# Two diffusion-transformer layers on one core: 16-bit sums of squares, the first FFN scales in one go, and three other paces

## The chip, the cores and the metric

One core of one Trainium2 chip. The metric is device time in microseconds (us) of the whole program, one launch. Engines are named as in the profile: PE (TensorE matmuls), PEld (its weight loads), DVE (VectorE), ACT (ScalarE), POOL (GpSimd), SP (SyncE, which issues most DMAs).

## The reference

Two layers over 1024 latent and 256 context tokens, width 1024, all in float32; in layer 0 the context tokens go through the same steps. Each layer normalizes and modulates, projects, runs windowed attention and a 2-D Fourier mixing side by side, projects out, and ends in a SwiGLU FFN of hidden width 2816.

```python
def fourier_mix(u, w_four):
    ...
    mixed = jnp.fft.fft2(ug, axes=(1, 3), norm='ortho').real.astype(u.dtype)
    return jnp.einsum('bngc,gcd->bngd', mixed, w_four).reshape(B, N, FOURIER_WIDTH)

def swiglu(h, w_gate, w_up, w_down):
    return (jax.nn.silu(h @ w_gate) * (h @ w_up)) @ w_down

def reference(...):
    for i in range(DEPTH):
        ...
        h = modulate(rmsnorm(x, norm_pre_mix[i]), sh1, sc1)
        p = h @ w_in[i]
        ...
        attn = windowed_gqa_with_context(q, k, v, kc, vc, sink[i])
        four = fourier_mix(u, w_fourier[i])
        mix = jnp.concatenate([attn, four], axis=-1) @ w_out[i]
        x_mid = x + g1 * rmsnorm(mix, norm_post_mix[i])
        hf = modulate(rmsnorm(x_mid, norm_pre_ffn[i]), sh2, sc2)
        x = x_mid + g2 * rmsnorm(swiglu(hf, w_gate[i], w_up[i], w_down[i]), norm_post_ffn[i])
        ...
```

## The kernel before

**Tiling.** Activations lie transposed, channels on the 128 partitions, tokens along the row, in two blocks: A and B of 640 tokens in layer 0, two of 512 in layer 1 (latent tokens alone). Float32 accuracy comes from splitting each operand into a high and a low part: three 16-bit matmuls (hi·hi, lo·hi, hi·lo) stand for each product of the FFN. The up product also uses a seven-product scheme on 2×2 halves, so each FFN weight pair needs four sums of its quarters, scaled by a power of two and split.

**FFN weights.** `load` reads the two 512 KB halves of one gate or up weight into the pool `raw` (four buffers). `start` adds, on ACT, the squares of each half (`junk`, L441; the sums land in `ss`). `factor` sums `ss` over the partitions with two float32 matmuls against ones (`wsum`, L420) and turns the result into the scale `sp` with three small DVE instructions (`power`, L410 to L412). `sums` then makes the four operands: ACT the high part (`wa` or `ww`, L457), DVE the low part (L458), with four additions of quarters between the second and the third (L469 to L472). The first four pairs, eight weights, are made ahead by `ahead`: for layer 0 beside its attention, for layer 1 beside the down product of layer 0. They are written to DRAM (`wc`) and read twice by `ffn_up`. The other weights, from pair 4 on, are made inside `ffn_up`, where `ready` calls `factor` and `wino`.

**What sets the order.** The program is written as generators. `mix` takes from several of them in turn: each has a total, and the next step comes from the one whose done share of its total is smallest. A larger total makes a generator run earlier. A scheduler then orders each engine's instructions, with program order as priority; engines work their rows in the resulting order, and PE, DVE, ACT, POOL and SP wait for each other at semaphores.

**Places that matter here.** In the attention of each layer three or four generators run together: `fill` (the rest of the projection, the Fourier mixing, the first half of the output projection; total FILL), `attn` (total ATT), in layer 0 `work` (the modulation matmuls, reading `wada`) and `early` (`ahead` of layer 0). In `fourier` each pass of first products (`v`, L955, and `vc`, L1003) is split by ACT and DVE (L909, L910) before the second products (`pq`, `fc`). At the start of `ffn_up`, block 0's products of the first four pairs run while `side` makes block 1's operands: `postnorm` of block 1, its statistics (`ssq`, then the matmul `nps`, L665), the spread of the scale over partitions (`rps`, L687), and `prenorm` (`hn`, then `ffn`, L743 and L744). Later in layer 0's `ffn_up`, `mod(0, 1)` makes layer 1's modulation on DVE (`wm`, L643). The down product (`acc<-…,wd`, L1215) converts its weights on the way: `wd` by ACT (L1207) and DVE (L1208), from the same four `raw` buffers.

## Time and profile before

| | us |
|---|---|
| median of 3 runs | 2600.11 (2595.58 to 2609.46) |
| the profiled execution | 2605.76, its span 2604.0 |
| PE busy | 2412.8 (93% of the span) |
| DVE busy | 1790.5 (69%) |
| ACT busy | 1347.3 (52%) |
| POOL busy | 196.9 (8%) |
| DMA | 390.06 MB, mean 150 GB/s |

The stages of the span, from the first and last matmuls of each line: up to 185 us the modulation and the first projections of layer 0; to 545 its attention, with Fourier's first products from 333 on; to 603 the second output projection; to 1158 the FFN up product; to 1505 the down product; then layer 1: projections to 1572, attention to 1863, output projection to 1915, up product to 2345, down product and the tail to 2604. Busy times of different engines overlap. A row of waits names the engine that waited and what released it. The granted clock is a share of full speed.

### The profile page before, as it was taken

To read this page: it belongs to the slowest core of one execution; us is meant where nothing else is said; L and a number is where in the kernel's file an instruction comes from. 1 tells how busy PE (TensorE), PEld (TensorE's weight loads), DVE (VectorE), ACT (ScalarE), POOL (GpSimd) and SP (SyncE) were. 2 spreads that over 40 slices of the span, in tenths; PEclk is the share of its full clock that TensorE was granted. 3 is DMA by queue.
4 is the path that set the end of the run, shared out by engine and by line. 5 is a ranking of instruction groups with operands and counts; after the bars stand their busy time and mean duration, and the time that the engine had idled before them with its cause. 6 is when DMAs were issued, how large, how long until landed. Compare 5 with 4: busy or idle time off the path is not lost.

```text
span 2604.0 us, 44237 instructions
## 1 busy us (share of the span) xinstructions
PE 2412.8 (93%) x17370; PEld 1935.6 (74%) x17370; DVE 1790.5 (69%) x3474; ACT 1347.3 (52%) x2587; POOL 196.9 (8%) x204
## 2 busy tenths in 40 slices
PE   7989988998989999988998989999999999999997
PEld 5878777896667677655665779988777888884486
DVE  5687686777556887765568478787767477765485
ACT  4565556567334445434456336566574355545473
POOL 0212110010000000000000024310000000000000
PEclk9989989999989999998999989999999999999998
DMA  8433323477634333357557141101396521236374
GB/s 299 152 109 103 106 74 108 162 239 278 209 131 146 106 108 122 122 195 269 198 192 273 64 141 61 45 25 33 109 333 237 180 82 66 81 103 232 117 256 128
DMA packets 152769, 390.06 MB, mean 150 GB/s; under 512 B 16976, under 2 KB 33776, under 8 KB 152560
## 3 DMA queue, kind: packets, MB, share of 16 engines
q1 hardware_dynamic: 143344, 372.55, 42.2%
q10 hardware_dynamic: 9216, 14.68, 1.6%
q8 instruction: 136, 2.23, 0.3%
q14 instruction: 73, 0.60, 0.1%
HBM read 322.41 MB, written 64.76 MB: 149 GB/s over the span
## 4 chain that ended last, share of the span: by engine, by line
PE 48%; DVE 10%; issue 4%; DMA 4%; ACT 3%; SPq 0%; POOL 0%; POOLq 0%; ACTq 0%; DVEq 0%
PE p L1084 21%; PE acc L1215 17%; PE accn L516 4%; PE acc L516 2%; DMA wm<-in_wada 1%; PE pv L245 1%; PE tp L229 1%; DVE X L710 1%; DMA raw<-in_wdown 1%; DMA hid<-hs 1%; DVE wm L643 1%; DVE ww L458 1%; DVE ssq L659 1%; PE score L201 1%; DVE lo L401 1%
## 5 line engine op out<-in xcount | busy, mean ns | idle before, releaser
L1084 PE MATMUL p<-ffn,ww 128*128 128x320 f16 (+1 forms) x7392 | 934.9, 288 | 39.4 <-ACT ffn L743 17.8
L1084 PEld LDWEIGHTS <-ww 128*128 128x128 f16 x7392 | 728.0, 99 | 237.8 <-issue 36.9
L1215 PEld LDWEIGHTS <-wd 128*128 128x128 f16 x3696 | 366.4, 100 | 197.5 <-ACT wd L1207 23.3
L1215 PE MATMUL acc<-hid,wd 128*128 128x320 f16 (+2 forms) x2544 | 343.5, 297 | 18.1 <-ACT wd L1207 13.0
L1208 DVE SCALAR_TENSOR_TENSOR wd<-raw,dn,wd 128x256 f16<-128x256 f32 x440 | 186.1, 480 | 132.6 <-ACT wd L1207 132.4
L516 PE MATMUL accn<-arena,hi 128*128 128x320 f32 (+1 forms) x992 | 255.8, 331 | 3.6 <-DVE arena L720 1.8
L1207 ACT ACTIVATE wd<-raw,dn 128x256 f16<-128x256 f32 x440 | 186.4, 495 | 93.6 <-PE acc L1215 68.6
L516 PE MATMUL acc<-arena,hi 128*128 128x320 f32 (+2 forms) x928 | 210.0, 332 | 3.9 <-ACT X L1038 2.7
L1215 PE MATMUL acc<-X,wd 128*128 128x320 f16 (+1 forms) x1152 | 200.9, 337 | 9.7 <-ACT wd L1207 6.4
L516 PEld LDWEIGHTS accn<-arena,hi 128*128 128x128 f32 x992 | 176.2, 194 | 13.0 <-DVE arena L720 3.3
L516 PEld LDWEIGHTS acc<-arena,hi 128*128 128x128 f32 x928 | 156.1, 192 | 19.6 <-issue 4.4
L516 PE MATMUL accn<-arena,lo 128*128 128x320 f32 (+1 forms) x496 | 162.1, 329 | 0.1
L672 POOL TENSOR_TENSOR nr<-nm,mhalf 128x5 f32<-128x5 f32 (+2 forms) x17 | 19.2, 1128 | 1782.6 <-DVE nm L671 1782.6
L457 ACT ACTIVATE ww<-raw,sp 128x1024 f16<-128x1024 f32 x112 | 110.4, 1034 | 83.3 <-DVE raw L472 50.6
L458 DVE SCALAR_TENSOR_TENSOR ww<-raw,sp,ww 128x1024 f16<-128x1024 f32 x112 | 125.5, 1147 | 35.9 <-ACT ww L457 35.6
L401 DVE TENSOR_TENSOR lo<-raw,hi 128x1024 fp32r<-128x1024 f32 x77 | 101.2, 1315 | 56.2 <-ACT hi L400 42.0
L245 PE MATMUL pv<-arena 128*128 128x256 f32 x518 | 118.5, 309 | 15.8 <-ACT arena L233 7.5
L233 ACT CAST arena<-tp 128x512 fp32r<-128x512 f32 (+1 forms) x184 | 96.6, 530 | 62.7 <-PE tp L229 61.3
L216 ACT ACTIVATE A<-score,ng 128x641 f32<-128x641 f32 (+2 forms) x144 | 106.7, 742 | 41.4 <-DVE ng L215 23.4
L516 PE MATMUL acc<-arena,lo 128*128 128x320 f32 (+2 forms) x464 | 126.0, 329 | 0.4 <-DVE lo L401 0.4
L215 DVE TENSOR_REDUCE ng<-score 128x1 f32<-128x641 f32 (+2 forms) x144 | 105.8, 740 | 29.5 <-PE score L208 28.6
L400 ACT CAST hi<-raw 128x1024 fp32r<-128x1024 f32 x77 | 80.6, 1046 | 85.4 <-PE acc L516 31.8
(229 smaller groups left out, 3765.0 us busy)
## 6 DMA issues: line engine op xcount, KB each, us to landing
raw<-in_wdown SPq DMA_DIRECT2D x112, 512.0 KB, 4.7
ww<-wc SPq DMA_DIRECT2D x96, 512.0 KB, 4.2
wm<-in_wada SPq DMA_DIRECT2D x96, 256.0 KB, 4.3
raw<-in_wgate SPq DMA_DIRECT2D x44, 512.0 KB, 4.3
raw<-in_wup SPq DMA_DIRECT2D x44, 512.0 KB, 4.7
raw<-in_wdown SPq DMA_DIRECT2D x56, 384.0 KB, 4.3
raw<-in_win SPq DMA_DIRECT2D x40, 512.0 KB, 3.5
wada<-in_wada SPq DMA_DIRECT2D x39, 512.0 KB, 4.2
```

The costliest lines, as they stand in the source:

```text
L215: nc.vector.tensor_reduce(self.ng[:, hs], sv, axis=AX.X, op=ALU.max, negate=True)
L216: nc.scalar.activation(p, sv, AF.Exp, bias=self.ng[:, hs], accum_out=self.su[:, hs])
L233: nc.scalar.copy(ph, tp[:, 0:256 * n])
L245: nc.tensor.matmul(self.pv[:, 0:256], net.V[:, self.kts[k], self.g, :], pt[:, 256 * i:256 * i + 256], start=(k == 0 and e == 0), stop=(k = ...
L401: nc.vector.tensor_tensor(lo[:, 0:w], raw[:, 0:w], hi[:, 0:w].bitcast(F32), op=ALU.subtract)
L457: nc.scalar.activation(hi, src, AF.Copy, scale=s)
L458: nc.vector.scalar_tensor_tensor(lo, src, s, hi, op0=ALU.mult, op1=ALU.subtract)
L516: self.nc.tensor.matmul(ps, wt[:, ks], xt[:, a:b], start=(k == 0 and i == 0), stop=(k == n - 1 and i == 2))
L1084: nc.tensor.matmul(ps, w[:, at:at + P], G[:, k, x, c, 0:h], start=(start and k + t == 0), stop=(k == KD // 2 - 1 and t == 2), skip_group_c ...
L1207: nc.scalar.activation(wt[:, 0, c], raw[:, c], AF.Copy, scale=r)
L1208: nc.vector.scalar_tensor_tensor(wt[:, 1, c], raw[:, c], r, wt[:, 0, c], op0=ALU.mult, op1=ALU.subtract)
L1215: nc.tensor.matmul(out, wt[:, e, k], xs[x][:, s, u:v], start=(f + s + i == 0), stop=(f == NP - 1 and s == 1 and i == 2))
```

## The change

Six edits.

1. `factor` handles a range `a` to `b` of weights. DVE adds the two columns of `ss` into a 16-bit tile `sq`, and one 16-bit matmul against ones (`bf1`) sums it over partitions, in place of two float32 matmuls per weight.
2. The first eight weights of a layer get their scales together: the new generator `norms` runs `start` for all eight and then one `factor` over eight columns. `ahead` no longer squares; it reads each weight again (`load`) when it makes the operands. For layer 0 `norms` stands ahead of `ahead` in `early`; for layer 1 it runs in the last part of layer 0's `ffn_up`, and `ahead` alone stays in the down product. The eight weights of a layer, 16 reads of 512 KB, are so read twice.
3. The totals of `ahead` are set to its new 24 steps: 32 with `norms` for 40 in the attention, 16 steps for 28 in the first half of the down product.
4. `fourier`: a step of first products counts 1.9 for 0.9; FILL goes from (160, 123) to (173, 131).
5. `side` in the first part of `ffn_up`: 45 for 27.
6. `first` (post-normalization of layer 0's block 1) in layer 1's first projections: 8 for 12.

```diff
-FILL = (160, 123)
+FILL = (173, 131)
...
-    def factor(self, l, i):
+    def factor(self, l, a, b):
         nc = self.nc
-        ps = self.ps.tile([P, 2 * NP], F32, tag="ps", name="wsum")[:, 0:1]
-        for j in range(2):
-            nc.tensor.matmul(ps, self.ones, self.ss[:, j, i:i + 1], start=(j == 0), stop=(j == 1))
-        self.power(self.sp[l][:, :, i:i + 1], ps.bitcast(I32), 24, 204)
-        if i >= 2 * AHEAD:
-            self.back(l, i, i + 1)
+        sq = self.sm.tile([P, 2 * AHEAD], BF16, tag="sq", name="sq")[:, 0:b - a]
+        nc.vector.tensor_tensor(sq, self.ss[:, 0, a:b], self.ss[:, 1, a:b], op=ALU.add)
+        ps = self.ps.tile([P, 2 * NP], F32, tag="ps", name="wsum")[:, 0:b - a]
+        nc.tensor.matmul(ps, self.bf1[:], sq, start=True, stop=True)
+        self.power(self.sp[l][:, :, a:b], ps.bitcast(I32), 24, 204)
+        if a >= 2 * AHEAD:
+            self.back(l, a, b)
+
+    def norms(self, l):
+        for i in range(2 * AHEAD):
+            self.start(l, i)
+            yield
+        self.factor(l, 0, 2 * AHEAD)
...
-        raw = self.start(l, 0)
         for i in range(2 * AHEAD):
-            yield
-            yield
-            self.factor(l, i)
-            yield from self.sums(l, i, raw, out, True)
-            raw = self.start(l, i + 1) if i + 1 < 2 * AHEAD else None
+            yield from self.sums(l, i, self.load(l, i), out, True)
...
                 self.split(*H(2 * p + e), ps[:])
-                yield 0.9
+                yield 1.9
...
         first(0)
-        yield 0.9
+        yield 1.9
         for p in range(4):
             if p < 3:
                 first(p + 1)
-                yield 0.9
+                yield 1.9
...
-                self.factor(l, i)
+                self.factor(l, i, i + 1)
...
-                mix((self.inproj(l, 0, (6, 7, 8)), cost(3, KD, BW - C)), (first, 12))
+                mix((self.inproj(l, 0, (6, 7, 8)), cost(3, KD, BW - C)), (first, 8))
...
-            early = self.ahead(l) if l == 0 else iter(())
-            mix((fill, FILL[l]), (self.attn(l, queries), ATT[l]), (work, 17), (early, 10 * AHEAD))
+            early = chain(self.norms(l), self.ahead(l)) if l == 0 else iter(())
+            mix((fill, FILL[l]), (self.attn(l, queries), ATT[l]), (work, 17), (early, 8 * AHEAD))
...
-            mix((part(up, 14 * AHEAD - 2), 2 * AHEAD * one), (side, 27))
+            mix((part(up, 14 * AHEAD - 2), 2 * AHEAD * one), (side, 45))
...
-            mix((up, one * (44 - 4 * AHEAD)), (mod(0, 1), 64))
+            mix((up, one * (44 - 4 * AHEAD)), (mod(0, 1), 64), (iter(()) if last else self.norms(l + 1), 2 * AHEAD))
...
-                mix(down(0, 0, w, first), (part(pre, 7 * AHEAD), 7 * AHEAD), (side, 32))
+                mix(down(0, 0, w, first), (part(pre, 4 * AHEAD), 4 * AHEAD), (side, 32))
```

How this moves instructions, at three places (a row is line, operation, what it writes and reads, size; `x4` is a count of equal rows). First ACT at the start of layer 0's down product; `wd` are the down weights, `wa` and `wc` those of layer 1 and their copy, `junk` the squares, `sp` the scale. Before:

```order
L1207 ACTIVATE wd<-raw,dn_118 128x256 x8
L441 ACTIVATE junk,ss<-raw 128x1024 x2
L457 ACTIVATE wa<-raw,sp_112 128x1024
L457 ACTIVATE wa<-raw,sp_112 128x512
L1207 ACTIVATE wd<-raw,dn_118 128x256 x3
```

And after:

```order
L1210 ACTIVATE wd<-raw,dn_118 128x256 x4
L465 ACTIVATE wa<-raw,sp_112 128x1024
L465 ACTIVATE wa<-raw,sp_112 128x512
L1210 ACTIVATE wd<-raw,dn_118 128x256 x4
L470 DMA wc<-wa 128x1024
```

The squares are gone from the down product, and with them the `wsum` on PE that stood between the squares and `wa`: PE's rows hold 1198 matmuls of line 1215 (now 1218) in a run, where a `wsum` stood behind the first 84 and then after every 60 to 270 more.

Second, DVE in the first part of layer 0's `ffn_up`; `hn` are the first rows of block 1's operands, `nm`, `ne` and `nr` the norm's scale, and the `A<-A,p` rows empty PSUM of block 0's products. Before:

```order
L1115 SCALAR_TENSOR_TENSOR A<-p_6792,inv_122,A 128x320
L675 TENSOR_TENSOR ne<-ne,nm 128x5
L676 TENSOR_SCALAR ne<-ne 128x5
L677 TENSOR_TENSOR nr<-nr,ne 128x5
L1103 TENSOR_TENSOR A<-A,p_6793 128x320
L1107 SCALAR_TENSOR_TENSOR A<-A,inv_122 128x960
L710 SCALAR_TENSOR_TENSOR hn<-X,fsc_107,r 128x640 x5
L1120 TENSOR_REDUCE hm<-A 128x1
```

And after:

```order
L1103 TENSOR_TENSOR A<-A,p_6456 128x320
L677 TENSOR_TENSOR ne<-nr 128x5
L678 TENSOR_TENSOR ne<-ne,nm 128x5
L1094 TENSOR_TENSOR A<-A,p_6584 128x320
L679 TENSOR_SCALAR ne<-ne 128x5
L680 TENSOR_TENSOR nr<-nr,ne 128x5
L1106 TENSOR_TENSOR A<-A,p_6456 128x320
L713 SCALAR_TENSOR_TENSOR hn<-X,fsc_107,r 128x640 x5
L1103 TENSOR_TENSOR A<-A,p_6584 128x320
```

`hn` stood behind the last additions of block 0's eight weights and now stands among those of the sixth. On PE the spread `rps` stood behind product 672 of 672 and now stands behind 470; the statistics `nps` stood behind 636 and now behind 396. In layer 1 `rps` goes from 600 to 420.

Third, PE at Fourier's first products in layer 0; `v` are these products, `tp` and `pv` those of attention (transposes and values). Before:

```order
L955 MATMUL v_3268<-A,X 128x128 x4
L229 MATMUL tp<-cst,A 128x128 x4
L955 MATMUL v_3282<-A,X 128x128 x2
L955 MATMUL v_3282<-A 128x128 x2
L229 MATMUL tp<-cst,A 128x128 x4
L955 MATMUL v_3319<-A,X 128x128 x4
```

And after:

```order
L958 MATMUL v_3142<-A,X 128x128 x4
L229 MATMUL tp<-cst,A 128x128 x6
L245 MATMUL pv<-arena_391 128x256 x5
L197 LDWEIGHTS bf_100
L197 MATMUL score<-sink,bf_100 128x1
L201 MATMUL score<-arena_391,qs 128x384
```

Between two passes of `v` there were some four transposes; now there is about a turn of attention. Over all of the `v` passes 11 value matmuls (`pv`) stood before and 33 do now.

## The prediction

> **What bounds the kernel now.** I read the page's head first, then busy time by stage, then what ended the waits in the stages that lose time.
>
> ```profile
> span 2604.0 us, 44237 instructions
> ...
> PEclk9989989999989999998999989999999999999998
> ```
>
> The span is 2604.0 us; this execution took 2605.76 us, 5.65 more than the median shown (2600.11). I make the sum against this execution and shift it by that difference at the end; half a per cent, 13 us, is about what a measurement of this kernel can tell from no change. The PEclk row (granted TensorE clock in 40 slices) has many nines: time is lost in small pieces, by idleness and by the reduced clock that follows.
>
> The view by stage has, after the stretch and its length, busy us and count for PE, PEld, DVE, ACT and POOL, the granted clock, the DMA share and GB/s. The rows are: attention of layer 0; start and rest of its FFN up product; its down product with the preparation of layer 1's first weights beside it, and after that has ended; start and rest of layer 1's up product.
>
> ```profile
> 185.00:545.00 360.00, 325.32 (x2210) 285.12 (x2206) 261.24 (x483) 209.81 (x437) 47.86 (x58) 0.95 0.36 121
> 603.00:740.00 137.00, 117.90 (x796) 80.78 (x795) 93.09 (x159) 68.30 (x116) 2.34 (x2) 0.91 0.57 197
> 740.00:1163.00 423.00, 408.52 (x2996) 292.88 (x2994) 304.05 (x607) 175.89 (x272) 0.00 (x0) 1.00 0.41 134
> 1163.00:1412.00 249.00, 220.68 (x1494) 151.91 (x1494) 158.35 (x333) 119.19 (x218) 3.30 (x2) 0.92 0.67 234
> 1412.00:1505.00 93.00, 93.00 (x688) 67.24 (x686) 44.82 (x95) 40.73 (x83) 0.00 (x0) 1.00 0.37 122
> 1915.00:2022.00 107.00, 95.82 (x815) 81.51 (x814) 78.48 (x162) 60.99 (x120) 2.02 (x2) 0.95 0.71 255
> 2022.00:2345.00 323.00, 322.63 (x2965) 289.23 (x2964) 215.61 (x397) 158.93 (x268) 0.00 (x0) 1.00 0.32 104
> ```
>
> TensorE bounds nearly everything; DVE and ACT have room in every stage. The two halves of the down product are the same work, yet one loses 8% of its clock and 28 us of PE time and the other nothing. Its matmuls alone (line 1215; PE, PEld, clock, DMA):
>
> ```profile
> 1163.00:1412.00 249.00, 214.60 (x1433) 144.41 (x1433) 0.92 0.67 234
> 1412.00:1505.00 93.00, 92.62 (x682) 66.44 (x679) 1.00 0.37 122
> ```
>
> 682 in 93 us is 0.136 us each; 1433 at that pace are 195.4 us, and they took 249: **53.6 us lost**, the largest loss of the profile, 34.4 of it idle (249 − 214.6) and the rest clock. Who waited there, from the list of waits (us in all, times, longest) and one round of it in order of time (start, length, then idle time before and what ended it):
>
> ```profile
> ACT wa L457 <- DVE sp L411: 44.3, 7, 12.6
> ACT wa L457 <- DVE raw L472: 35.4, 10, 6.5
> DVE pe L410 <- PE wsum L420: 26.5, 10, 7.0
> ```
>
> ```profile
> 1243.99 0.50 PE L420 MATMUL wsum<-ss,cst 128*128 128x1 f32 x4
> 1244.35 5.05 PE L1215 MATMUL acc<-X,wd 128*128 128x320 f16 x36
> 1244.53 0.16 DVE L410 TENSOR_SCALAR pe<-wsum 128x1 int32<-128x1 int32 x1 [5.19 <-PE wsum L420]
> 1244.91 1.76 ACT L457 ACTIVATE wa<-raw,sp 128x1024 f16<-128x1024 f32 x2 [8.07 <-DVE sp L411]
> 1252.58 0.71 PE L1215 MATMUL acc<-hid,wd 128*128 128x320 f16 x2 [3.17 <-ACT wd L1207]
> ```
>
> It is a circle. ACT stands 8.07 us before `wa`, because the scale `sp` comes from DVE, which waits 5.19 us for the sum `wsum`, which stands in PE's queue behind the matmuls. Behind `wa` on ACT stand the `wd` weights; so PE, having passed `wsum`, runs out of them and idles 3.17 us.
>
> **The change, part by part.**
>
> *Scales in one go, layer 1 (moved out of the down product).* The eight pairs' squares now run during the up product and one `wsum` of 8 columns follows; in the down product no `wsum` is left, and `wa` waits for no scale. Of ACT's waits ahead of `wa` the scale is 44.3 of 79.7 us, 56%; the waits for the sums on DVE (L472) stay. 56% of 53.6 is 30. From that I take 5, because `raw` is now read at the time of use and no longer one pair ahead, so ACT can meet the read; the first bubble, at the start of the product with the 28 reads of `hid` around it, also stays in part. Bounds: 13 (if the reads replace half of the waits) and 45. I take **−25**.
>
> The price is in layer 0's up product: 16 reads of 512 KB more, 16 squares, 16 accumulator reads, all new there. Rows of such a square, and of its read (KB each, us to landing):
>
> ```profile
> L441 ACT ACTIVATE junk<-raw 128x1024 bf16<-128x1024 f32 x88 | 92.5, 1052 | 43.0 <-DMA raw<-in_wup 25.1 <-DMA raw<-in_wgate 14.0 <-issue 1.4
> L441 ACT ACTIVATION_READ_ACCUMULATOR junk<-raw 128x1 f32 x88 | 16.6, 189 | 0.0
> raw<-in_wgate SPq DMA_DIRECT2D x44, 512.0 KB, 4.3
> raw<-in_wup SPq DMA_DIRECT2D x44, 512.0 KB, 4.7
> ```
>
> 16 × (1.05 + 0.19) is 20 us of ACT, beside 175.89 busy of 423: hidden, if ACT doesn't stand. Behind a square that waits for its read stand ACT's copies out of PSUM, for which PE waits; on SP, the reads for `wm` stand behind these. So far ACT waited 39.1 us for 88 squares, 0.44 each; 16 such are 7. Bounds: 0, and 16 × (4.5 + 1.24) = 92, every landing and square laid bare. I take **+5**, near the measured 0.44.
>
> *One bf16 matmul for each `wsum`.* What one costs where PE is dense, from three neighbours in layer 1:
>
> ```profile
> 2069.83 3.77 PE L1084 MATMUL p<-ffn,ww 128*128 128x256 f16 x33
> 2073.43 0.50 PE L420 MATMUL wsum<-ss,cst 128*128 128x1 f32 x4
> 2073.80 1.47 PE L1084 MATMUL p<-ffn,ww 128*128 128x256 f16 x12
> ```
>
> From `wsum` to the next start are 0.37 us. The new one is a single 16-bit pass; as one more matmul of the stream it would cost a step of about 0.11 (3.60 us over 33). Bounds 0 and 0.37; I take 0.12. 28 in the two up products × 0.25 = **−7**. Each gains a DVE addition ahead of it (the 1-column row L410 above took 0.16 us), 28 × 0.16 = 4 us of a DVE that is busy 304 of 423 us: hidden. The seven `power` triples saved in each layer weigh as much the other way.
>
> *Normalization of block 1 paced at 45 instead of 27.* In layer 0 its statistics were ready on DVE at 667.9, but stand in PE's order at 702, and the transpose `rps` behind the last product of block 0:
>
> ```profile
> 666.12 1.74 DVE L659 TENSOR_TENSOR ssq<-ssq,sq 128x640 f32<-128x640 f32 x2
> 702.27 0.28 PE L665 MATMUL nps<-cst,ssq 128*128 128x1 f32 x2
> 708.11 0.71 PE L687 MATMUL rps<-cst,nr 128*128 128x128 f32 x5
> 709.96 4.06 DVE L710 SCALAR_TENSOR_TENSOR hn<-X,fsc,r 128x640 f32<-128x640 f32 x5
> 725.89 1.23 PE L1084 MATMUL p<-ffn,ww 128*128 128x320 f16 x4 [5.37 <-ACT ffn L743]
> ```
>
> Line 1084 alone (us, PE, PEld, clock, DMA):
>
> ```profile
> 708.00:736.00 28.00, 15.98 (x63) 8.12 (x62) 0.70 0.08 27
> 740.00:1157.00 417.00, 404.62 (x2931) 286.72 (x2930) 1.00 0.40 130
> 1993.00:2021.00 28.00, 22.59 (x185) 18.48 (x183) 0.94 0.38 132
> ```
>
> 63 matmuls in 28 us, at 0.136 they are 8.6: 19.4 lost. Now `rps` stands ahead of the last 202 products of block 0, 27 us of cover, and the operands took 708 to 736, 28 us, to make. The first `nps` stood behind product 636, at 702.27; now it stands behind product 396, 240 × 0.136 earlier, at 669.6, 1.7 us after the statistics were ready: that wait just fits. What comes late instead: the five `hn` on DVE (4.06 us in the last row but one) now stand ahead of additions that empty PSUM. I take **−15** (bounds −19 and 0). In layer 1, 185 in 28 us at 0.109 are 20.2: 7.8 lost; the cover rises from 72 products to 252; **−5** (0 to −7).
>
> *Attention.* During Fourier's first products PE waited (same columns as by stage):
>
> ```profile
> 330.00:363.00 33.00, 25.19 (x151) 21.92 (x150) 27.62 (x50) 18.59 (x38) 8.75 (x10) 0.79 0.33 119
> 1716.00:1742.00 26.00, 24.05 (x173) 20.94 (x171) 23.38 (x50) 17.20 (x39) 8.94 (x12) 0.93 0.07 21
> ```
>
> Layer 0 loses 7.8 idle and 21% of 33, 6.9, by clock: 14.7. The larger step puts 33 value matmuls of attention where 11 stood, but attention uses the same DVE, busy 27.62 of 33: I take 6, and 1 of the 3.8 in layer 1. FILL grows by 13 and 8, for 12 and 8 of added steps, so the rest moves by little. Eight `wsum` become one: 8 × 0.37 − 0.12 = 2.8. Against it the 16 squares of layer 0 stand together early, and 16 reads are new: +2. In sum **−8** (−20 to +10). The pace 8 for 12 leaves DVE's rows at layer 1's start as they are, and PE's but for one matmul: nothing.
>
> **Sum:** −25 + 5 − 7 − 15 − 5 − 8 = −55. 2605.76 − 55 = 2550.8 as profiled, 2545 against the median.
>
> **A rule weighed.** Is the clock's part won back with the gaps? The rows of one small gap (PE, PEld, DVE, ACT, POOL, clock):
>
> ```profile
> 1279.00:1282.20 3.20, 1.30 (x9) 0.72 (x9) 3.20 (x6) 2.85 (x6) 0.00 (x0) 0.99 0.67 241
> 1282.20:1285.60 3.40, 3.40 (x15) 1.96 (x13) 2.91 (x5) 0.39 (x1) 0.00 (x0) 0.50 0.44 149
> ```
>
> 1.9 us idle in 3.2, and the next 3.4 us ran at 0.50. So here small gaps cost clock, and my terms count it. The Trainium skill ("TensorE: Matmul & The Clock Gate", section "HAM oscillation — how this bites in real kernels") gives as the rule no gaps above some 3.4 us. By that rule gaps this short would leave the clock alone, and closing them would not win it back; this row speaks against it.
>
> **The rivals.**
> - *Clock not won back.* Only idle time returns: of 25, 34.4/53.6, 16; of 15, 12.0/19.4, 9; of 5, 5.4/7.8, 3.5; of the 8, some 4.5. 20 less: 2565. The two rows above speak against it. (The page on the clock gate named above would have it so.)
> - *The circle closes by another way.* ACT waits for the read of `raw`, then for DVE's sums; PE gains 13 instead of 25, and the squares cost 14 instead of 5: −34, 2566. For it: 35.4 us of L472 remain and four `raw` buffers are shared with the `wd` reads.
> - *More is won.* Down product −40, attention −18, squares 0: 15 + 10 + 5 more, 2515. For it: the second half of the down product, with no preparation, loses nothing.
> - *Attention suffers.* The 16 new reads take `raw` buffers from w_in and w_ada; at half a landing each, 2.25 us, 36, and the 8 not won: 2589, no change. Against it: DMA share 0.36 there.
> - *Slower:* the squares in layer 0's up product stop ACT, and PE has little slack: 2931 matmuls at 0.136 are 399 of 417 us. At the full price of 92 instead of 5: 2632. It undoes the gain from (55 + 5)/16 = 3.8 us for each read, and is slower by 0.5% from 4.6; the 0.44 measured speaks against it.
>
> **How the numbers follow.** Forecast 0.48, with a range of its own of 2528 to 2562 from the down term (13 to 33) and the attention's; circle 0.18; more won 0.14; clock 0.06; attention 0.08; slower 0.06. The first four are faster by over 13 us: 0.86; the fifth within: 0.08; the last slower: 0.06. The range from 2520 to 2580 leaves out attention and slower and a little of more won: 0.18.
>
> **What would show it.** Right: no wait of `wa` for `sp` and no `wsum` between 1163 and 1500; line 1215's matmuls with clock above 0.96 over the down product; a single PE gap of under 3 us around the start of block 1 in either layer; `wsum` with 30 matmuls instead of 176. Wrong: `wa` waiting for DMA by 30 us or more; ACT's squares ending PSUM's waits between 800 and 1157, PE below 0.95 there; line 955 still waiting for DVE as long; the loss at 708 only moved to `rps` waiting for DVE.

## Result and profile after

The changed kernel took **2522.34 us** (median of 4 runs, 2519.76 to 2523.33) against 2603.82 for the kernel before on the same chip: ratio 0.9688, 95% interval 0.9657 to 0.9718, so about 81 us faster. The profiled execution took 2523.14 us, 82.6 less than that of before. The head of its page:

```profile
span 2521.3 us, 44064 instructions
...
PEclk9998989999999999998999989999999999999998
```

The difference is worked out by stage. A stage runs from the first matmul of one kind to the first of the next, as the timeline of PE has them; the rest of an up product ends with its last matmul. Each kernel has one profile, so a stage time is one measurement. In layer 0's attention the kernel before and `pace45` (below) have the same order on PE, and took 449.1 and 445.9 us: 3 us in one stage can be chance. In us:

| stage | before | after | difference |
|---|---|---|---|
| layer 0, attention and Fourier, up to the output projection | 449.1 | 440.7 | −8.4 |
| output projection | 58.3 | 54.8 | −3.5 |
| up product, block 0 (first 672 matmuls) and next 588 | 109.6, 95.2 | 103.2, 79.9 | −6.4, −15.3 |
| rest of the up product | 349.5 | 354.7 | +5.2 |
| down product, first and second block | 178.9, 162.2 | 153.1, 151.0 | −25.8, −11.1 |
| layer 1, attention and Fourier | 291.4 | 284.9 | −6.4 |
| up product: 672, 588, rest | 86.9, 71.7, 271.3 | 86.2, 64.9, 268.9 | −0.8, −6.9, −2.4 |
| everything else | | | −0.8 |

All but one stage became shorter. First the down product's matmuls (line 1218, before 1215; us, PE, PEld, clock, DMA share, GB/s), first and second block:

```profile
1135.00:1289.00 154.00, 148.07 (x1056) 104.67 (x1057) 0.96 0.89 311
1289.00:1440.00 151.00, 145.59 (x1057) 103.92 (x1055) 0.99 0.44 147
```

The first block now takes nearly as long as the second, with 5.9 us idle (154 − 148.07). The waits of ACT that stood ahead of `wa` and `wd`, over the whole program (line 465 was 457, 480 was 472, 1210 was 1207):

```profile
ACT wd L1210 <- DMA raw<-in_wdown: 42.3, 21, 9.0
...
ACT wa L465 <- DVE raw L480: 13.0, 6, 5.6
...
ACT wa L465 <- DMA raw<-in_wup: 10.4, 8, 3.2
...
ACT wa L465 <- DVE sp L411: 4.7, 1, 4.7
```

The wait for the scale fell from 44.3 us to a single one of 4.7, which lies in layer 0's attention. The wait for the sums (line 480) fell as well, from 35.4 to 13.0 (in the down product from 33.4 to 6.9), though nothing in the change touches the sums. ACT now waits for reads instead, 42.3 us before `wd` (24.4 before the change) and 10.4 before `wa`. One sign that the prediction named for being wrong is there, `wa` waiting for DMA by 30 us or more: all such waits, other transfers than reads of `raw` included, are 32.1 us over the program, 21.5 of them in the down product. Yet PE does not follow: its matmuls there wait 4.2 us for ACT's `wd`, 18.9 before. ACT is ahead of PE, and stands longer until PE has done with an earlier `wd` (down product of layer 0, before and after):

```profile
ACT wd L1207 <- PE acc L1215: 14.2, 4, 5.2
```

```profile
ACT wd L1210 <- PE acc L1218: 31.7, 7, 7.0
```

The start of block 1 in both layers' up products (line 1087, before 1084; same columns), and the sums of squares:

```profile
680.00:708.00 28.00, 28.00 (x208) 20.16 (x207) 1.00 0.47 155
775.00:1130.00 355.00, 338.22 (x2439) 237.42 (x2436) 1.00 0.44 142
1929.00:1994.00 65.00, 64.52 (x592) 57.61 (x590) 1.00 0.65 211
```

```profile
L421 PE MATMUL wsum<-sq,bf 128*128 128x1 bf16 (+1 forms) x30 | 5.0, 167 | 1.0 <-DVE A L1118 1.0
```

```profile
656.19 1.17 PE L668 MATMUL nps<-cst,ssq 128*128 128x1 f32 x10
...
667.27 0.71 PE L690 MATMUL rps<-cst,nr 128*128 128x128 f32 x5
667.81 42.41 PE L1087 MATMUL p<-ffn,ww 128*128 128x320 f16 x311
```

Where 63 matmuls stood in 28 us at a clock of 0.70, 208 stand at 1.00; the statistics `nps` come at 656, `rps` at 667, and the products run on without a gap. Of 176 matmuls for the sums thirty are left.

Last, Fourier's first products in layer 0, all engines (PE, PEld, DVE, ACT, POOL):

```profile
318.00:365.00 47.00, 35.18 (x228) 28.57 (x227) 38.28 (x69) 28.12 (x57) 9.89 (x12) 0.85 0.42 140
```

This stretch is longer than before (47 us for 33, with more of attention in it) and still has 11.8 us of idle PE and a clock of 0.85. Its `v` waits for DVE no less, first before (4.1 us), then now (5.7 in two rows):

```profile
PE v L955 <- DVE arena L910: 4.1, 2, 2.5
```

```profile
PE v L958 <- DVE arena L913: 3.6, 2, 2.2
...
PE v L958 <- DVE arena L234: 2.1, 1, 2.1
```

That was another of the prediction's signs of being wrong: the cure meant for this stretch did not reach it.

### The profile page after: what moved, and what is told of

Same layout as the page of the kernel before. It is cut to its first block, busy times and chain, and to the rows that moved or that the text cites. A ratio compares the mean times of both kernels' runs of the same rounds, so it can differ in the third digit from the quotient of the medians.

```text
span 2521.3 us, 44064 instructions
## 1 busy us (share of the span) xinstructions
PE 2366.0 (94%) x17224; PEld 1906.6 (76%) x17224; DVE 1789.1 (71%) x3462; ACT 1346.8 (53%) x2587; POOL 197.3 (8%) x204
## 5 line engine op out<-in xcount | busy, mean ns | idle before, releaser
L1087 PE MATMUL p<-ffn,ww 128*128 128x320 f16 (+1 forms) x7392 | 923.3, 287 | 28.4 <-ACT ww L465 6.2
L1218 PE MATMUL acc<-hid,wd 128*128 128x320 f16 (+2 forms) x2544 | 337.2, 295 | 4.1 <-ACT wd L1210 3.8
L1218 PE MATMUL acc<-X,wd 128*128 128x320 f16 (+1 forms) x1152 | 194.0, 330 | 0.6 <-ACT wd L1210 0.6
L449 ACT ACTIVATE junk<-raw 128x1024 bf16<-128x1024 f32 x88 | 92.4, 1052 | 46.7 <-DMA raw<-in_wup 21.8
```

Source lines behind the costliest of these rows:

```text
L1087: nc.tensor.matmul(ps, w[:, at:at + P], G[:, k, x, c, 0:h], start=(start and k + t == 0), stop=(k == KD // 2 - 1 and t == 2), skip_group_c ...
L1218: nc.tensor.matmul(out, wt[:, e, k], xs[x][:, s, u:v], start=(f + s + i == 0), stop=(f == NP - 1 and s == 1 and i == 2))
```

## The experiments

Each kernel's ratio is against the kernel before, timed on the same chip in the same rounds; stages are those of the table.

### The parts, each by itself

The scales and the 16-bit sums alone (the yields at three places in `fourier`):

```diff
-FILL = (173, 131)
+FILL = (160, 123)
...
-                yield 1.9
+                yield 0.9
...
-                mix((self.inproj(l, 0, (6, 7, 8)), cost(3, KD, BW - C)), (first, 8))
+                mix((self.inproj(l, 0, (6, 7, 8)), cost(3, KD, BW - C)), (first, 12))
...
-            mix((part(up, 14 * AHEAD - 2), 2 * AHEAD * one), (side, 45))
+            mix((part(up, 14 * AHEAD - 2), 2 * AHEAD * one), (side, 27))
```

> The changed kernel with block 1's operands paced at 27, FILL at (160, 123), Fourier's yields at 0.9 and `first` at 12, as before: only the scales in one go and the 16-bit sums are left of the change. If the parts are independent, this kernel keeps what the stages of the scales won (the first down product went from 341.1 to 304.1 us, 36.9 less; the rest of layer 0's up product after its first 1260 products rose from 349.5 to 354.7) and some 5 us of cheaper sums: 35 to 42 us under before, about 2563. If instead the gain of the down product came from the other pacing (block 1 earlier, so that less is left behind it), its first half stays near 179 us instead of 153 and the kernel is at 2585 or above.

Measured: 2544.84 us, ratio 0.9793 (0.9776 to 0.9811). The down product won 30.3 (152.2 and 158.6 us) and block 1's start nothing, so most of the down product's gain, and all of it in the first block, is not the pacing's. The 7.6 us by which the second block stays behind the changed kernel stand at its `rps`, which waits 9.8 us for its statistics on DVE, 2.7 in the changed kernel. Layer 0's attention went to 432.5 us, 16.6 less, twice what the whole change wins there; that is most of the 18 us by which the kernel is faster than expected.

Only the pace of block 1's operands, in the kernel before:

```diff
-            mix((part(up, 14 * AHEAD - 2), 2 * AHEAD * one), (side, 27))
+            mix((part(up, 14 * AHEAD - 2), 2 * AHEAD * one), (side, 45))
```

> Before, with the pace of block 1's operands alone changed from 27 to 45. Independent parts: the first 1260 products of layer 0's up product lose 18 to 22 us of their 204.8 and those of layer 1 6 to 8 of their 158.6, so 24 to 30 us under before, about 2577, with the down product unchanged at 341 us. Rival: of the 21.7 us that these stages lost in layer 0, part is the cheaper sums and a busier clock from the other edits; then 12 to 16 in layer 0, and 2588.

Measured: 2573.75, ratio 0.9903 (0.9882 to 0.9924), so 25 us. The two stages around the start of block 1 won 3.6 and 15.0 us in layer 0, 1.6 and 7.2 in layer 1; the down product stayed at 342.2. The parts are independent here, as the first expectation had it.

Only Fourier's steps (at three places) and FILL in the kernel before, and as `fill_only` the change of FILL alone:

```diff
-FILL = (160, 123)
+FILL = (173, 131)
...
-                yield 0.9
+                yield 1.9
```

> Before, with FILL (173, 131) and Fourier's yields at 1.9 alone. By the sum of the prediction: 6 and 1 us less in the two attentions, 2596. By the stages of the changed kernel, if none of their gain is due to the norms that went to the attention of layer 0: 8 us less in layer 0 and 6 less in layer 1, so 2589. If the gain in layer 0 came from the wsum and not from the pacing, 2597 with layer 0 unchanged.

> Before, with FILL (173, 131) for (160, 123) alone; Fourier's steps stay at 0.9. With both edits (`fourier`), layer 1's attention up to its output projection went from 291.4 to 285.7 us, 5.7 less, of which 5.3 ahead of Fourier and 9.5 behind it, with 7.7 given back in it. If the gain ahead of Fourier is FILL's (other work taken at another pace beside attention), it shows here, 4 to 6 us; if it is only the places of Fourier's steps, layer 1 stays at 291 and the kernel at 2600. Layer 0 is expected within 5 us of its 449.1 either way.

Measured: 2590.19, ratio 0.9961 (0.9947 to 0.9976), with both; 2587.68, ratio 0.9952 (0.9935 to 0.9969), with FILL alone. By stage: with both, layer 0 won 1.7 us and layer 1 5.7; with FILL alone 6.9 (the expectation allowed 5) and 8.1. So the gain is FILL's, and the longer Fourier steps add nothing or take some back. One profile of each can't fix the size of that.

Only the 16-bit sums, squares and scales at their old places:

```diff
-        for j in range(2):
-            nc.tensor.matmul(ps, self.ones, self.ss[:, j, i:i + 1], start=(j == 0), stop=(j == 1))
+        sq = self.sm.tile([P, 2 * AHEAD], BF16, tag="sq", name="sq")[:, 0:b - a]
+        nc.vector.tensor_tensor(sq, self.ss[:, 0, a:b], self.ss[:, 1, a:b], op=ALU.add)
...
+        nc.tensor.matmul(ps, self.bf1[:], sq, start=True, stop=True)
```

> Before, with only the sum over partitions in 16 bits: one matmul per weight instead of two float32 ones, squares and scales at their old places. By the prediction's sum: 28 sums in the up products times 0.25 us, 7 us, and 2592; by the dense row of the changed kernel, 28 x 0.34, 9.5 us. If the float32 sum itself was what held the scale back in PE's queue, the down product also gains (its 7 in the first half, 0.37 us each, 2.6 us, and the waits that hang on them): 5 us or more of its 178.9, and 2585. If the attention's gain in `scales` (16 us in layer 0) came from the sums being short, it shows here too; if it came from the squares going first, attention stays at 449 us.

Measured: 2592.19, ratio 0.9964 (0.9951 to 0.9977). The rest of the two up products won 6.5 and 2.3 us. The down product stayed at 178.0 and 161.3, attention at 451.8: the form of the sum is not what held either of them. In the first block of the down product (lines 458 and 411 are the old 457 and 411) `wa` still stands for the scale:

```profile
ACT wa L458 <- DVE sp L411: 40.5, 5, 11.9
```

### Which link of the circle cost the time

The down product's gain has several candidates: the scale in PE's queue, the squares' work on ACT, or the chain of the two. First the scale alone was to go back into it, pair by pair; the squares stay in the up product:

```diff
     def norms(self, l):
         for i in range(2 * AHEAD):
             self.start(l, i)
             yield
-        self.factor(l, 0, 2 * AHEAD)
+        if l == 0:
+            self.factor(l, 0, 2 * AHEAD)
...
     def ahead(self, l):
...
         for i in range(2 * AHEAD):
+            if l > 0:
+                self.factor(l, i, i + 1)
             yield from self.sums(l, i, self.load(l, i), out, True)
```

> The changed kernel, but in layer 1 the scale of each early pair is again made on its own, ahead of its sums in the first down product; the squares and their reads stay in the up product, and nothing else differs. Circle theory: what cost the time was the scale that stands in PE's queue between ACT's `wa` and DVE; then it returns, the first half of the down product (153.1 us) goes back by 15 to 27 us and the kernel to 2540 to 2550. Rival, moved work: it was the 8 squares and 8 reads on ACT and SP taken out of the down product (28 to 35 us of ACT and 4 MB); then the time stays within 5 us of 2522.

This expectation errs on one point: the reads did not leave the product. The changed kernel reads these weights twice, and the down product's own 16 reads remain; the squares that left it are 16, two for each of the eight weights.

Measured: 2532.85, ratio 0.9745 (0.9730 to 0.9759), 10.5 us over the changed kernel, which fits neither theory. Its line 1221 is that of the down product (same columns):

```profile
1136.00:1289.00 153.00, 147.98 (x1057) 104.64 (x1058) 0.97 0.89 314
1289.00:1453.00 164.00, 147.07 (x1057) 103.36 (x1055) 0.96 0.40 134
```

The first block stays at 152.3 us. But the scales did not go back to their old places. In `bf16_only` the eight stand on PE behind 84, 264, 456, 648, 756, 1020, 1200 and 1320 matmuls of the product; here, with the squares long ready, the order put six ahead of its first matmul (at 1136.63), one behind 96 and one behind 1224:

```profile
1134.71 0.48 PE L421 MATMUL wsum<-sq,bf 128*128 128x1 bf16 x4
1135.80 0.16 PE L421 MATMUL wsum<-sq,bf 128*128 128x1 bf16 x1 [0.61 <-DVE pe L410]
1136.32 0.16 PE L421 MATMUL wsum<-sq,bf 128*128 128x1 bf16 x1 [0.35 <-DVE pe L410]
...
1154.58 0.18 PE L421 MATMUL wsum<-sq,bf 128*128 128x1 bf16 x1
...
1312.77 0.17 PE L421 MATMUL wsum<-sq,bf 128*128 128x1 bf16 x1
```

All the loss is in the second block, 163.7 against 151.0, and in it almost all in one place. ACT first, then PE:

```profile
1313.36 1.76 ACT L466 ACTIVATE wa<-raw,sp 128x1024 f16<-128x1024 f32 x2 [5.52 <-DVE sp L411]
...
1326.52 0.74 ACT L661 ACTIVATE ssq<-X 128x640 f32<-128x640 f32 x1 [9.23 <-DVE X L786]
```

```profile
1334.69 0.71 PE L1221 MATMUL acc<-hid,wd 128*128 128x320 f16 x2 [11.33 <-ACT wd L1213]
```

The last pairs' `wa` now stand behind the start of block 0's normalization on ACT, where in the changed kernel they had ended at 1298. There the scale is waited for, then the normalized `X`, and PE runs out of `wd` for 11.33 us. So the run does not show what eight scales in PE's queue cost with old squares: in the first block one stands there, and no `wa` waits for it. It shows that scales with old squares need not stand there, and that the last one, which does, again makes `wa` wait.

Next the squares go back alone, in layer 1, at the old places and in the old steps, with nothing hanging on them:

```diff
     def ahead(self, l):
...
+        raw = self.start(l, 0) if l else None
         for i in range(2 * AHEAD):
-            yield from self.sums(l, i, self.load(l, i), out, True)
+            if l:
+                yield
+                yield
+            yield from self.sums(l, i, raw if l else self.load(l, i), out, True)
+            raw = self.start(l, i + 1) if l and i + 1 < 2 * AHEAD else None
...
-                mix(down(0, 0, w, first), (part(pre, 4 * AHEAD), 4 * AHEAD), (side, 32))
+                mix(down(0, 0, w, first), (part(pre, 7 * AHEAD), 7 * AHEAD), (side, 32))
```

> The changed kernel, but layer 1's early pairs are squared a second time in the first down product, at the places and in the steps of before (read one pair ahead, square, two empty steps, sums, 7 x AHEAD steps). Nothing uses the second squares: the scales come from the first ones, so `wa` waits for no scale; reads are as before (16) there. Theory A, the chain of before (read, square, sum over partitions, scale, `wa`): squares without the scale hanging on them are harmless, as PE ran at 1.00 beside ACT's squares from 1152 to 1172 in `norms_in_down`; first half of the down product (153.1 us) 150 to 158, the kernel 2518 to 2528. Theory B, work on ACT: 16 squares and accumulator reads, 20 us, ahead of the `wd` in ACT's order cost what they cost before; first half 168 to 179, the kernel 2540 to 2550. In between, 160 to 167: both.

Measured: 2523.90, ratio 0.9705 (0.9692 to 0.9718), no loss that the interval separates from the changed kernel. The down product's first block took 148.0 us, the second 156.8 (153.1 and 151.0 in the changed kernel). All engines in the first (PE, PEld, DVE, ACT, POOL, clock, DMA, GB/s):

```profile
1137.00:1286.00 149.00, 147.53 (x1062) 104.73 (x1063) 106.10 (x220) 84.00 (x157) 0.00 (x0) 0.98 0.80 284
```

```profile
ACT wa L465 <- DVE raw L480: 19.1, 4, 6.9
...
ACT junk L449 <- DMA raw<-in_wgate: 13.6, 4, 5.9
...
ACT junk L449 <- DMA raw<-in_wup: 7.2, 5, 2.7
```

The squares are there, with their waits for reads (20.8 us), and so is a wait for the sums; PE is busy 147.5 of 149 us. ACT's work is not the cause, nor are these waits. `bf16_only`, with the same squares at the same places and the scale hanging on them, took 178.0. So what costs is the scale that hangs on fresh squares: `wa` stands until its sum has passed PE's queue.

Two differences from the changed kernel remain. The first block is 5.1 us shorter, because the empty steps put off the first `wa`: the kernel is 5.4 us ahead after 300 matmuls, as `late_start` below is by 6.1, and keeps the changed kernel's pace from there. The second block is 5.8 us longer, because `rps` waits 8.0 us there for 2.7; in `late_start`, which squares nothing in the down product, it waits 6.6.

Then both, but in one go, at the head of the down product:

```diff
-            mix((up, one * (44 - 4 * AHEAD)), (mod(0, 1), 64), (iter(()) if last else self.norms(l + 1), 2 * AHEAD))
+            mix((up, one * (44 - 4 * AHEAD)), (mod(0, 1), 64))
...
-                pre, side = self.ahead(l + 1), mod(2)
-                mix(down(0, 0, w, first), (part(pre, 4 * AHEAD), 4 * AHEAD), (side, 32))
+                pre, side = chain(self.norms(l + 1), self.ahead(l + 1)), mod(2)
+                mix(down(0, 0, w, first), (part(pre, 6 * AHEAD), 6 * AHEAD), (side, 32))
```

> The changed kernel, but layer 1's eight norms (16 reads, 16 squares, then one scale for all) stand at the head of the first down product instead of in layer 0's up product. Two theories on the 25 to 27 us that the first half of the down product won. Moved work: what mattered is that 20 us of ACT and 8 MB of reads left that product; then they cost it again, its first half (153.1 us) goes to 168 to 180 and the kernel to about 2540, less the 5 to 8 us that the up product gets back. Chain per pair: what mattered is that read, square, sum, scale and weight no longer follow each other pair by pair through four queues; then squares in one go are cheap there too, the first half stays within 8 us, the up product gets 5 to 8 us back, and the kernel stays at 2517 to 2527.

Here the 16 reads come on top of the product's own; the expectation speaks of them as if they had left it.

Measured: 2541.36, ratio 0.9766 (0.9752 to 0.9781). The rest of the up product took 343.5 us, 11.2 less than in the changed kernel; the first block of the down product 175.7, 22.6 more; the second 160.6, 9.6 more, where `rps` waits 12.3 us. By its number this is what moved work would give, but the trace says otherwise:

```profile
1152.00:1172.00 20.00, 20.00 (x150) 14.42 (x148) 7.68 (x20) 14.88 (x30) 0.00 (x0) 1.00 0.95 353
```

```profile
1139.68 1.06 ACT L449 ACTIVATE junk<-raw 128x1024 bf16<-128x1024 f32 x1 [12.46 <-DMA raw<-in_wup]
...
1188.65 1.76 ACT L465 ACTIVATE wa<-raw,sp 128x1024 f16<-128x1024 f32 x2 [13.10 <-DVE sp L411]
```

```profile
1172.58 0.16 DVE L419 TENSOR_TENSOR sq<-ss 128x8 bf16<-128x8 f32 x1
```

```profile
1141.46 8.78 PE L1218 MATMUL acc<-X,wd 128*128 128x320 f16 x48 [8.56 <-ACT wd L1210]
...
1172.89 13.20 PE L1218 MATMUL acc<-X,wd 128*128 128x320 f16 x96
1185.93 0.17 PE L421 MATMUL wsum<-sq,bf 128*128 128x8 bf16 x1
...
1206.44 0.71 PE L1218 MATMUL acc<-X,wd 128*128 128x320 f16 x2 [6.22 <-ACT wd L1210]
```

With ACT 74% busy between squares and `wd`, PE runs at 20.0 of 20 us. It stops twice. At the start a square met a late read (8.56). The changed kernel idles at its start too, 9.3 us from 1130 to 1160 where this one idles 10.3 from 1122 to 1152, and after 300 matmuls this kernel is only 4.6 us behind. The next 100 matmuls, around the one scale, lose 16.8 us more: `sq` is ready on DVE at 1172.7, `wsum` stands behind 96 matmuls in PE's queue until 1185.9, and `wa` stands 13.10 us for the scale. The longest stop there, 6.22 us, is not the scale's alone: ahead of that `wd` ACT also stood 6.5 us for the modulation on DVE and 3.0 for the sums. So eight scales in one go behind fresh squares are one such wait instead of eight, and a long one. The first theory had the size, though not for its reason; neither had the reads.

### Towards a better version

The old pacing of attention for layer 0 alone:

```diff
-FILL = (173, 131)
+FILL = (160, 131)
...
-                yield 1.9
+                yield 1.9 if l else 0.9
```

> The changed kernel with the old pacing of attention in layer 0 (FILL 160, Fourier's yields 0.9) and the new one in layer 1 (131, 1.9). The kernel `scales` had 432.5 us from layer 0's first scores to the output projection, the changed kernel 440.7, and the one with Fourier's pacing alone won 1.7 of 449.1. If the two edits disturb each other in layer 0, this kernel is 5 to 8 us faster than the changed one, about 2516. If the 8 us are the variation of one execution, it is within 3 us of 2522.

Measured: 2514.35, ratio 0.9657 (0.9638 to 0.9676); the interval overlaps the changed kernel's. By stage the answer is clearer. Layer 0's attention took 440.7, 437.7, 439.6, 437.3 and 443.0 us in the five kernels that have the norms first and the new pacing (the changed one, `one_by_one`, `norms_in_down`, `late_start`, `squares_again`), and 432.5, 435.7, 431.8 and 434.8 in the four with the norms first and the old pacing (`scales`, `split_pace`, and `both` and `norms_fine` below): 439.7 against 433.7 on the mean, and no overlap, though the nearest two are 1.6 us apart. The two edits disturb each other there by some 6 us.

A head start for the down product:

```diff
-                mix(down(0, 0, w, first), (part(pre, 4 * AHEAD), 4 * AHEAD), (side, 32))
+                main, n = down(0, 0, w, first)
+                t = 0
+                while t < 16:
+                    t += next(main)
+                mix((main, n - t), (part(pre, 4 * AHEAD), 4 * AHEAD), (side, 32))
```

> The changed kernel, with the first 16 units (some 120 matmuls) of the first down product ahead of the preparation of layer 1's weights and its modulation. From 1130 to 1160 the changed kernel has 9.3 us of idle PE and a clock of 0.79, with the DMA share at 1.04. If the reads of the preparation delay the first `wd` there, 5 to 10 us come back, 2514. Rival: the 28 reads of `hid` alone fill the DMA, and the preparation ends later and meets the first outputs of the second block; then no change, or 5 us more.

Measured: 2515.36, ratio 0.9663 (0.9649 to 0.9678), again overlapping. All engines at the start of the product, in the changed kernel and in this one:

```profile
1135.00:1160.00 25.00, 20.11 (x115) 12.46 (x116) 16.89 (x37) 10.52 (x20) 0.00 (x0) 0.77 1.04 392
```

```profile
1129.00:1160.00 31.00, 29.92 (x201) 20.48 (x200) 18.95 (x44) 13.20 (x28) 0.00 (x0) 0.89 0.99 376
```

The bubble is gone (147.0 us for the first block, 6.1 less), but 4.0 of it are given back in the second, where `rps` now finds its statistics late:

```profile
1309.33 1.30 PE L690 MATMUL rps<-cst,nr 128*128 128x128 f32 x5 [6.57 <-DVE nr L680]
```

In the changed kernel that wait is 2.71 us. Net, 2 us by stage; the rest of the 7 between the medians is not this edit's by anything that the trace shows.

Both together, and the norms of layer 1 in finer steps on top:

```diff
     def norms(self, l):
...
         for i in range(2 * AHEAD):
-            self.start(l, i)
+            if l == 0:
+                self.start(l, i)
+                yield
+                continue
+            raw = self.load(l, i)
             yield
+            for j in range(2):
+                junk = self.tmp.tile([P, 1024], BF16, tag="t", name="junk")
+                self.nc.scalar.activation(junk[:], raw[j][:], AF.Square, accum_out=self.ss[:, j, i:i + 1])
+                yield
...
-            mix((up, one * (44 - 4 * AHEAD)), (mod(0, 1), 64), (iter(()) if last else self.norms(l + 1), 2 * AHEAD))
+            mix((up, one * (44 - 4 * AHEAD)), (mod(0, 1), 64), (iter(()) if last else self.norms(l + 1), 6 * AHEAD))
```

> `split_pace` and `late_start` in one kernel: layer 0's attention paced as before, layer 1's as in the changed kernel, and the first 16 units of the first down product alone. If the two are independent, 8 us and 7 us under the changed kernel: 2507. If the second is given back at the start of the second block (its `rps` waited 6.5 us there), 2510 to 2514.

> As `both`, with the norms of layer 1 in layer 0's up product in finer steps: the two reads one step ahead of the first square, and one square in each step instead of two. The norms cost 11 us there (354.7 against 343.5 in `norms_in_down`). If that is ACT standing 2.5 us, and longer where it meets the read, ahead of its copies out of PSUM, half of it or more comes back: 5 to 8 us under `both`. If it is the work and the reads themselves (DMA, PSUM's turns), no change within 2 us.

Measured: `both` **2507.39**, ratio 0.9641 (0.9628 to 0.9654), below the changed kernel's interval: the best version here, 94 us under before. `norms_fine` took 2519.24, ratio 0.9680 (0.9659 to 0.9702); the rest of its up product took 361.5 us against 353.1 in `both`. The finer steps cost 8 us where 5 to 8 were to be won. Squares waiting for reads and additions waiting for squares, `norms_fine` first (its lines 457 and 419), then `both`:

```profile
DVE sq L419 <- ACT junk L457: 16.1, 6, 6.8
ACT junk L457 <- DMA raw<-in_wup: 16.1, 10, 3.6
...
ACT junk L457 <- DMA raw<-in_wgate: 12.5, 8, 2.6
```

```profile
ACT junk L449 <- DMA raw<-in_wup: 13.5, 7, 3.6
DVE sq L419 <- ACT junk L449: 6.2, 3, 4.1
...
ACT junk L449 <- DMA raw<-in_wgate: 3.3, 1, 3.3
```

The reads come later to the squares, not earlier. That more `raw` buffers are held for longer, which four buffers shared with the reads of the up product would make likely, is argued and not shown.

## Why the prediction was right in its sign and short in its size

The forecast was 2545 us, −55, and −82.6 came in the profiled execution, −81 between the medians. 2522 lies inside the range given and outside the forecast's own 2528 to 2562, next to the rival "more is won" (2515). Term by term:

- **Scales in one go, −25: measured −36.9 in the whole change, −30.3 alone (`scales`).** The place was right, and so was the sign that `wa` would stop waiting for `sp`. The step that failed is "56% of 53.6": it split the loss among ACT's waits as if each stood by itself, and left the waits for the sums their share. They shrank with it, in the down product from 33.4 to 6.9. In a circle the wait that an engine shows is where the circle stops it, not a share that stays when another is cut. The other 6.6 us lie in the second block and are partly luck: the wait of `rps` in the second block is between 2.2 and 12.3 us in the eight kernels that make all scales in one go, no edit aims at it, and the changed kernel has 2.7 where `scales` has 9.8. `squares_again` shows the other half: a wait for the sums (19.1 us) and for reads (20.8) can stand there without costing PE anything.
- **The mechanism held.** The prediction put the cost on a sum that stands in PE's queue. `squares_again` has the squares without a scale on them and loses nothing in the first block (148.0 us); `bf16_only` and `norms_in_down`, with scales behind fresh squares, take 178.0 and 175.7 there. Whether eight scales spread over PE's queue would cost as much with old squares is not shown, since `one_by_one` has but one of them in that block. The prediction speaks of two halves of the down product, but its 53.6 us run to 1412, 70 us into the second block, so that block's 11.1 us belong to the same term. There the order counts too: in `one_by_one`, and in the kernel before (`wa` at 1404, behind `sq`, and 3.17 us of idle PE behind it), the last `wa` fall into the next normalization.
- **Price in the up product, +5: measured 11.2** (354.7 against 343.5 without the norms), inside the bounds of 0 and 92. 0.70 us for each read and square instead of the 0.31 taken; the rate of 0.44 waited for each square so far left out what PE then waits in turn: its products idle 16.8 us there (355 − 338.22), and 9.2 without the norms (344 − 334.78, `norms_in_down`). The slower rival would have needed 4.6 us each. Under the old pacing the norms cost less: `scales` has 349.9 us there and `bf16_only`, without them, 343.0.
- **The sums in 16 bits, −7: measured −8.8** (6.5 and 2.3). The new matmul was taken at a stream's step of 0.12 us and costs less:

```profile
2044.78 4.86 PE L1087 MATMUL p<-ffn,ww 128*128 128x256 f16 x43
2049.47 0.17 PE L421 MATMUL wsum<-sq,bf 128*128 128x1 bf16 x1
2049.50 4.75 PE L1087 MATMUL p<-ffn,ww 128*128 128x256 f16 x42
```

  0.03 us from its start to the next, 0.37 before; 28 × 0.34 is 9.5.
- **Block 1's pace, −15 and −5: measured −18.6 and −8.8** alone (`pace45`), −21.7 and −7.7 in the whole change. In the whole, 19.4 us were lost at 708 and all returned; `nps` at 656 and `rps` at 667 stand in the stream without a wait, and the five `hn` on DVE stop nothing.
- **Attention, −8 for both layers: measured −8.4 and −6.4, and not for the reasons given.** The 6 us for Fourier's steps failed: the stretch idles 11.8 us of 47 where it idled 7.8 of 33, with 0.85 for a clock of 0.79, and `fill_only` wins as much without the steps. FILL, put at nothing ("the rest moves by little"), is what wins in layer 1. The four kernels with the old pacing there took 286.9 to 291.4 us, 289.6 on the mean; the nine with the new one 282.5 to 286.7, 284.2 on the mean; FILL alone 283.3. In layer 0 the gain belongs to the norms in one go, with the second reads and the new totals that came with them, put at −2.8 + 2 and worth −16.6 in `scales`; the new pacing gives 6 back.
- **The clock is won back with the gaps.** The down product's matmuls before the change, first block alone (same columns as after):

```profile
1163.00:1342.00 179.00, 159.27 (x1052) 106.95 (x1053) 0.91 0.66 230
```

  PE's idle time in the block fell from 19.7 us to 5.9, 13.8 less, and its busy time for nearly the same matmuls by 11.2, from 159.27 to 148.07. The clock of 0.91 for 0.96 explains 8.3 of these (159.27 × (1 − 0.91/0.96)): a third of the 25.0 us that the two rows differ by is clock. The Trainium skill ("TensorE: Matmul & The Clock Gate", section "HAM oscillation — how this bites in real kernels") asks for no gaps above some 3.4 us. By it, as the prediction read it, the gaps would have left the clock alone and the 8.3 us would not have come back. The trace does not agree: PE's longest gap in that block before was 3.2 us (the last row of the prediction's round, at 1252), and closing the gaps raised the clock from 0.91 to 0.96. The waits of PE's matmuls for `wd` from ACT in the whole down product before (us, times, longest):

```profile
PE acc L1215 <- ACT wd L1207: 18.9, 11, 3.2
```

The rivals: the circle did not close through reads, though ACT's waits for them before `wd` rose from 24.4 to 42.3; attention did not suffer from the 16 reads; the squares cost 11 us, where the slower rival needed 74 (16 × 4.6).

## What to carry to other kernels

Where several engines wait in a circle, do not divide the loss among the waits shown: ask which link takes its input fresh from the link before, and take that one out of the loop, even at the price of reading twice. Test a link by putting it back alone: in the first block of the down product the squares cost nothing (148.0 us), and squares and scale in a row some 25 us (178.0 in `bf16_only`, 153.1 in the changed kernel). And look in the trace whether the edit put the link where it was meant to stand: in `one_by_one` six of eight scales had gone ahead of the product. And edits that were each paced against the same stage need a run together with one of them undone: here layer 0 was better without the new pacing, and the version that follows this and the head start (`both`) is 12 to 15 us faster than the change (by the ratios and by the medians).

## What the runs showed of the hardware

- A 16-bit matmul of one column in a dense stream costs 0.03 us from its start to the next (0.37 for the float32 pair), though its row says 0.17.
- The DMA share rose from 0.66 to 0.89 in the down product's first block, with 311 GB/s, and PE's clock and idle time got better, not worse. In its first 25 us PE was busy 20.1 at a share of 1.04; in `late_start`, where the product had a head start, it was busy 29.9 of 31 at 0.99. A share near one alone did not stop it.
- With ACT 74% busy for 20 us (`norms_in_down`) PE was busy all 20.0, and with ACT busy 84 of 149 us (`squares_again`) PE was busy 147.5. In the down products of these runs not how busy ACT was told whether PE waited, but what stood in front of `wd` in ACT's order.
